# RWKV-7 steps: py in turn with pu, and a brought into the scores' bank by products

## The chip, the cores and the metric

The kernel runs on one core of a Trainium2 chip. A core has five engines, each with its own queue of instructions: TensorE (PE in the profile; its weight loads are shown apart as PEld), VectorE (DVE), ScalarE (ACT), GpSimd (POOL) and SyncE (SP), which issues most transfers. The metric is the device time of one execution in microseconds. The kernel before has a median of 1361.54 us over three runs (1357.82 to 1363.87).

## The reference

A two-layer decoder trunk works on 512 tokens of width 1024 in float32: a recurrent block (RG-LRU), a gated conv-MLP, an RWKV-7 time-mixing block, a second gated conv-MLP, and a final norm. The change lies in the RWKV-7 block, and there in the recurrence over tokens. For each of 16 heads with a 64x64 state S:

```python
    def step(S, inp):
        r_t, w_t, k_t, v_t, a_t, b_t = inp
        sa = jnp.einsum('bhij,bhj->bhi', S, a_t)
        S = S * w_t[:, :, None, :] + sa[..., None] * b_t[:, :, None, :] + v_t[..., :, None] * k_t[..., None, :]
        y = jnp.einsum('bhij,bhj->bhi', S, r_t)
        return S, y
```

So each token's output y is the state after its own update, read out by r; the state decays by w, is fed with the outer product of v and k, and is corrected along b by what it gives for a.

## The kernel before

The program is one long list of instructions, in the order in which a scheduler has put them on each engine. Large projections run as three fp32r products of 512 columns each (lines 51 to 53). The recurrence is not run token by token. The 512 tokens are cut into 8 chunks of 64; inside a chunk everything becomes products of 64x64 blocks (`rwkv_chunks`).

The heads lie in two halves H (eight heads each), and each half in two groups g of four heads. `step(n, ...)` runs for n = 0 to 16. Step n does chunk n of group 0 and chunk n - 1 of group 1, counted through both halves (0 to 15, so that steps 0 and 16 have one group alone). The parity q of a chunk says which 64 partitions it uses; the two groups of a step have opposite parities, and so use opposite halves of the partitions. A loop over `heads` goes i (0, 1), h (0, 1), group.

What one step computes, with the names of tiles that the profile shows:

- `pe`: the product of `W` (the scores and a) with the state `sv`, which also holds v in its other half. ScalarE copies it to `e1` (line 1200).
- `py`, first part (line 1206): r times the state. It opens an accumulation that the end of the step closes. r comes from `rts`, a copy on the right partitions, or from `AR`.
- `prep_s(n + 1)`: the next step's scores, `s` (line 1150): for each head the 128x128 block of (b, k) against (a, r), 64 rows deep. VectorE multiplies them by `masks` into `W` (line 1157). One 64x64 block of each result is not wanted, since the inverse of the solve holds it already.
- `between` and `fill(0)`: one part of a finished tail, and background products of other work.
- `pu` (line 1216): the inverse `LT` times `e1`. ScalarE copies it to `u`, a part of the tile `tu` (line 1220).
- `prep_t(n + 1)`: transposes of b and k (`tr`, line 1164), copied to `tok` (also in `tu`); then ScalarE puts a into the unwanted block of `W` (line 1173, one copy for each group and h), r into `rts` (line 1175), and v into `tu`.
- `fill(1)`, then `pd`: the change of the state, from `tok` and `u` (line 1229). VectorE adds it to the state and multiplies by the decay (lines 1237 to 1240).
- `py`, second part (line 1243): `W` times `u` and v. ScalarE copies y to `ytok` (line 1247). Then `fill(2)`.

Every second step starts a tail for 128 finished tokens: a norm over each head on VectorE, ScalarE and GpSimd (lines 1257 to 1271), and then four transposes `pz` on TensorE ahead of the next step's `pe`. Background work comes from three lists (`fills` gives how much of each is put in at the three places): products of v's projection and of the gate, the solve of the second half of the heads, whose VectorE chain (lines 1038 and 1040) runs through the first four steps, and the first half of the output projection.

All small products are in float32, and each shows as two records in the profile. `tile_position` gives the row and the column of the 128x128 array where a product's weights lie. The scores lie at rows h * 64 and take all columns; `py` and `pu` take one 64x64 quarter each, and the two groups take opposite quarters; `pe` and `pd` take all rows and half of the columns. All PSUM tiles come from one rotation of 8 banks. The scheduler may move an instruction past others of its engine; `keep_in_program_order` forbids it for the instruction that it is given.

Of the kernel before, what the change touches and what calls it, by code (L numbers as in the profile page):

```python
# [15 lines left out]
P = 128  # L16
# [5 lines left out]
C = 64  # L22
# [19 lines left out]
class Kernel:  # L42
# [1039 lines left out]
    def rwkv_chunks(self, pool, mv, AR, BK, PC, selk, LTs, again):  # L1082
# [9 lines left out]
        nc, tc, I = self.nc, self.tc, self.I  # L1092
        V = self.x.rearrange("p k t -> p (k t)").rearrange("p (c n) -> p c n", c=4)
        half = lambda i: slice(i * 64, i * 64 + 64)

        svs = [pool.tile([P, 4, 2, C], F32, name=f"sv{i}") for i in range(2)]
        rts = pool.tile([P, 4, C], F32, name="rts")
        e1 = pool.tile([P, 2, 2, C], F32, name="e1")
# [9 lines left out]
        for q in range(3):  # L1108
            for e in range(2):
                for z in range(2):  # L1110
                    m = masks[half(e), q, z, :]
                    nc.gpsimd.affine_select(m, m, [[1, C]], ALU.is_gt if z != q % 2 else ALU.is_ge, 0.0, base=0, channel_multiplier=-1)
        sets, ytok = {}, {}
# [28 lines left out]
        def prep_s(n):  # L1142
            gs = groups(n)
            W = sets[n][0]
            pss = [four(self.bank("s")) for _ in range(2)]
            for i in range(2):
                for g, bs, H, c, c2, q in gs:
                    ch = slice(q * P, (q + 1) * P)
                    for h in range(2):
                        nc.tensor.matmul(pss[h][:, 2 * g + i, :], BK[H][half(h), 2 * g + i, c2, ch], AR[H][half(h), 2 * g + i, c2, ch],  # L1150
                                         start=True, stop=True, tile_position=(h * 64, 0))

            q0, g0, k = gs[0][5], gs[0][0], len(gs)
            mask = masks[:, q0 : q0 + k].rearrange("p q z t -> p q (z t)").unsqueeze(2).to_broadcast([P, k, 2, P])
            two = lambda t: t[:, 2 * g0 : 2 * (g0 + k)].rearrange("p (g i) t -> p g i t", i=2)
            for h in range(2):
                nc.vector.tensor_tensor(two(W[:, h]), two(pss[h]), mask, ALU.mult)  # L1157
        def prep_t(n):
            gs = groups(n)
            W, tok, uv = sets[n]  # L1160
            pt = four(self.bank("tr"))
            for g, bs, H, c, c2, q in gs:
                for i in range(2 * g, 2 * g + 2):
                    nc.tensor.transpose(pt[:, i, :], BK[H][:, i, c2, q * P : (q + 1) * P], self.ident)
            bs = slice(gs[0][1].start, gs[-1][1].stop)
            nc.scalar.copy(tok[:, bs], pt[:, bs])
            for g, bs, H, c, c2, q in gs:
                bh = half(1 - q)
                for h in range(2):

                    part = lambda z: AR[H][half(h), bs, c2, q * P + z * C : q * P + (z + 1) * C]

                    tc.keep_in_program_order(nc.scalar.copy(W[bh, h, bs, bh], part(1 - q)))
                    if h == q:
                        nc.scalar.copy(rts[bh, bs], part(q))
                n0 = H * 512 + g * 256
                v = V[half(q), c2, n0 : n0 + 256].rearrange("p (i t) -> p i t", t=P)
                nc.scalar.copy(uv[half(q), bs], v)
                nc.vector.tensor_copy(svs[n % 2][half(q), bs].rearrange("p i h t -> p i (h t)"), v)
# [5 lines left out]
        def step(n, between):  # L1185
            gs = groups(n)
            W, tok, uv = sets.pop(n)
            sv = svs[n % 2]
            more = n < 2 * NC

            heads = [(i, h, G) for i in range(2) for h in range(2) for G in gs]
            by_head = lambda ps: ps[:, 0:256].rearrange("p (i h t) -> p i h t", h=2, t=C)
# [3 lines left out]
            for i, h, (g, bs, H, c, c2, q) in heads:  # L1196
                bh = half(1 - q)
# [1 line left out]
            of = slice(0, P) if len(gs) == 2 else half(1 - gs[0][5])  # L1199
            nc.scalar.copy(e1[of], pe[of])  # L1200

            py = by_head(self.bank("py"))
            for i, h, (g, bs, H, c, c2, q) in heads:
                kh, bh, b = half(q), half(1 - q), 2 * g + i
                r = rts[bh, b] if h == q else AR[H][bh, b, c2, q * P + q * C : q * P + q * C + C]
                nc.tensor.matmul(py[kh, i, h], r, sv[bh, b, h], start=i + h == 0, stop=False,  # L1206
                                 tile_position=(64 - q * 64, q * 64))
            if more:
                prep_begin(n + 1)
                prep_s(n + 1)  # L1210
            between()
            fill(0)
            pu = by_head(self.bank("pu"))
            for i, h, (g, bs, H, c, c2, q) in heads:
                bh = half(1 - q)
                nc.tensor.matmul(pu[bh, i, h], LTs[H][bh, c2 * 8 + (2 * g + i) * 2 + h, :], e1[bh, i, h], start=True, stop=True,
                                 tile_position=(64 - q * 64, 64 - q * 64))
            for g, bs, H, c, c2, q in gs:
                bh = half(1 - q)
                nc.scalar.copy(uv[bh, bs], flat(pu[bh]))  # L1220
            if more:
                prep_t(n + 1)
            fill(1)
            if any(c < NC - 1 for g, bs, H, c, c2, q in gs):
                pd = by_head(self.bank("pd"))
                for i, h, (g, bs, H, c, c2, q) in heads:
                    if c < NC - 1:
                        b = 2 * g + i
                        nc.tensor.matmul(pd[half(1 - q), i, h], tok[:, b, half(h)], uv[:, b, half(h)], start=True, stop=True, tile_position=(0, 64 - q * 64))
                for g, bs, H, c, c2, q in gs:  # L1230
                    if c == NC - 1:
                        continue
                    kh, bh = half(q), half(1 - q)
                    Sn = svs[1 - n % 2][kh, bs]
                    w = decay[:, H * 4 + 2 * g : H * 4 + 2 * g + 2, :, c : c + 1].to_broadcast([P, 2, 2, C])
# [5 lines left out]
            for i, h, (g, bs, H, c, c2, q) in heads:  # L1241
                kh, b = half(q), 2 * g + i
# [261 lines left out]
```

## Time and profile before

| | before |
|---|---|
| median of three runs | 1361.54 us |
| profiled execution, its own time | 1359.88 us |
| its span in the profile | 1357.9 us |
| granted TensorE clock, mean over the span | 0.989 |
| the 17 steps | about 744 to 914 us of the span |
| TensorE, VectorE, ScalarE busy over the span | 1324.4, 863.6, 632.6 us |
| copies of a into W (line 1173) | 64, median 297 ns |
| mask products into W (line 1157) | 34, median 680 ns |

The profile is one execution. The time outside its span is 2.0 us. A row of the timeline gives start, length, engine, line, operation and tiles (output <- inputs), with the number of instructions merged in it and, in brackets, the idle time before it and what ended it. The chain of waits is the work that ended last, followed back from the end: a shorter instruction shortens the program only if it, or what it releases, stands on that chain. A busy engine in a stretch is not for that reason the limit there.

### The profile page before, as it was taken

What the parts mean: (1) busy time and instruction counts of PE and PEld (TensorE: products, weight loads), DVE (VectorE), ACT (ScalarE), POOL (GpSimd) and SP (SyncE); (2) the same over time, 40 slices, a digit from 0 to 9 for tenths busy, and PEclk for the clock granted to TensorE, in tenths of its full rate; (3) what the DMA queues carried; (4) which work ended last, traced back from release to release, by engine and by line L of the source; (5) the groups of instructions that cost most, each with busy time, mean ns of one, the idle gap of its engine ahead of it and who ended that gap; (6) DMA issues with size and microseconds to landing.
All of it is one profiled execution on the core that took longest, in us unless ns stands there. A gap on an engine that the chain in (4) does not pass through costs nothing.

```text
span 1357.9 us, 19301 instructions
## 1 busy us (share of the span) xinstructions
PE 1324.4 (98%) x7827; PEld 1068.8 (79%) x7827; DVE 863.6 (64%) x1332; ACT 632.6 (47%) x1032; POOL 68.8 (5%) x113
## 2 busy tenths in 40 slices
PE   8999999999999999999999988898999999999998
PEld 7877888888888888866679776676888888888886
DVE  5988756555354755597897975776646464365623
ACT  6797534333233523378636578653634242244311
POOL 4000000000000000020011011110000000000000
PEclk8999999999999999999999989998999999999999
DMA  5423333232333434222121111212333222334311
GB/s 182 119 62 93 109 94 109 79 104 67 106 94 94 143 93 125 63 72 79 62 86 49 58 33 64 56 60 65 109 93 94 77 93 78 109 94 126 122 63 62
DMA packets 72120, 120.20 MB, mean 89 GB/s; under 512 B 9498, under 2 KB 21476, under 8 KB 71904
## 3 DMA queue, kind: packets, MB, share of 16 engines
q1 hardware_dynamic: 70672, 117.20, 27.9%
q8 instruction: 61, 1.00, 0.3%
q10 hardware_dynamic: 576, 1.05, 0.2%
q0 software_dynamic: 784, 0.74, 0.2%
q14 instruction: 27, 0.22, 0.1%
HBM read 114.44 MB, written 4.52 MB: 88 GB/s over the span
## 4 chain that ended last, share of the span: by engine, by line
PE 89%; DVE 6%; ACT 2%; issue 1%; DMA 1%; POOL 1%; SPq 0%; POOLq 0%; ACTq 0%; DVEq 0%
PE acc L51 22%; PE acc L53 22%; PE acc L52 22%; PE acc L616 3%; PE acc L615 3%; PE acc L617 3%; PE acc L986 1%; PE s L1150 1%; PE pe L1198 1%; PE acc L987 1%; PE py L1206 1%; PE acc L988 1%; DVE W L1157 1%; PE ssq L915 1%; DMA xin<-in_x_dram 1%
## 5 line engine op out<-in xcount | busy, mean ns | idle before, releaser
L51 PE MATMUL acc<-xs,wh 128*128 128x512 f32 x896 | 352.1, 393 | 0.0
L53 PE MATMUL acc<-xs,wl 128*128 128x512 f32 x896 | 349.0, 390 | 0.7 <-DVE wl L91 0.7
L52 PE MATMUL acc<-xs,wh 128*128 128x512 f32 x896 | 349.5, 390 | 0.0
L91 DVE TENSOR_TENSOR wl<-raw,wh 128x1024 fp32r<-128x1024 f32 (+1 forms) x201 | 242.6, 1215 | 164.6 <-PE acc L52 90.1
L90 ACT CAST wh<-raw 128x1024 fp32r<-128x1024 f32 (+1 forms) x201 | 208.1, 1045 | 258.6 <-DVE wl L91 167.6
L53 PEld LDWEIGHTS acc<-xs,wl 128*128 128x128 f32 x896 | 168.5, 188 | 36.5 <-DVE wl L91 1.2
L51 PEld LDWEIGHTS acc<-xs,wh 128*128 128x128 f32 x896 | 168.8, 188 | 35.0 <-ACT wh L90 0.2
L52 PEld LDWEIGHTS acc<-xs,wh 128*128 128x128 f32 x896 | 168.7, 188 | 34.7 <-DVE wl L91 0.2
L576 DVE SCALAR_TENSOR_TENSOR cv<-gpad,pv,cv 128x512 f32<-128x512 f32 x96 | 71.8, 748 | 22.6 <-ACT cv L574 21.5
L90 ACT CAST hid<-un 128x512 fp32r<-128x512 f32 x48 | 29.8, 620 | 109.2 <-DVE un L583 109.1
L616 PE MATMUL acc<-wh,hid 128*128 128x512 f32 (+1 forms) x200 | 76.8, 384 | 0.0
L615 PE MATMUL acc<-wh,hid 128*128 128x512 f32 (+1 forms) x200 | 76.5, 382 | 0.0
L617 PE MATMUL acc<-wl,hid 128*128 128x512 f32 (+1 forms) x200 | 75.9, 380 | 0.0
L52 PE MATMUL acc<-hid,wh 128*128 128x512 f32 x192 | 75.7, 394 | 0.0
L53 PE MATMUL acc<-hid,wl 128*128 128x512 f32 x192 | 75.6, 394 | 0.0
L51 PE MATMUL acc<-hid,wh 128*128 128x512 f32 x192 | 75.5, 393 | 0.0
L582 DVE TENSOR_TENSOR un<-acc,rb 128x512 f32<-128x512 f32 x48 | 33.0, 688 | 43.5 <-PE acc L53 43.5
L91 DVE TENSOR_TENSOR hid<-un,hid 128x512 fp32r<-128x512 f32 x48 | 33.1, 690 | 32.0 <-ACT hid L90 32.0
L574 ACT ACTIVATE cv<-gpad,pv 128x512 f32<-128x512 f32 x48 | 39.2, 817 | 20.1 <-DVE gpad L571 19.9
L578 ACT ACTIVATE ge<-cv 128x512 f32<-128x512 f32 x48 | 30.1, 627 | 35.9 <-DVE cv L576 35.9
L620 DVE TENSOR_TENSOR xtok<-xtok,acc 128x512 f32<-128x512 f32 (+1 forms) x25 | 16.6, 665 | 45.6 <-PE acc L617 45.6
L615 PEld LDWEIGHTS acc<-wh,hid 128*128 128x128 f32 x200 | 37.5, 188 | 8.0
(424 smaller groups left out, 2207.6 us busy)
## 6 DMA issues: line engine op xcount, KB each, us to landing
raw<-in_ffn_w_up_dram SPq DMA_DIRECT2D x96, 512.0 KB, 3.9
raw<-in_ffn_w_down_dram SPq DMA_DIRECT2D x48, 512.0 KB, 3.8
raw<-in_rwkv_w_rkv_dram SPq DMA_DIRECT2D x24, 512.0 KB, 3.8
raw<-in_lru_w_in_dram SPq DMA_DIRECT2D x16, 512.0 KB, 3.9
raw<-in_lru_w_out_dram SPq DMA_DIRECT2D x8, 512.0 KB, 3.7
raw<-in_rwkv_w_out_dram SPq DMA_DIRECT2D x8, 512.0 KB, 3.5
xd<-x SPq DMA_DIRECT2D x8, 256.0 KB, 2.0
AR<-xd SPq DMA_DIRECT2D x1, 2048.0 KB, 8.8
```

The source lines that it names most:

```text
L51: nc.tensor.matmul(ps, wh, xh, start=start, stop=False)
L52: nc.tensor.matmul(ps, wh, xl, start=False, stop=False)
L53: nc.tensor.matmul(ps, wl, xh, start=False, stop=stop)
L90: (self.nc.vector.tensor_copy if dve else self.nc.scalar.copy)(hi, src)
L91: self.nc.vector.tensor_tensor(lo, src, hi.bitcast(F32), ALU.subtract)
L574: nc.scalar.activation(cv, gp[:, 0:T], AF.Identity, bias=self.vec(f"ffn_conv_b{l}", fb), scale=cw(0))
L576: nc.vector.scalar_tensor_tensor(cv, gp[:, j : j + T], cw(j), cv, ALU.mult, ALU.add)
L578: nc.scalar.activation(ges[o], cv, AF.Gelu_apprx_tanh)
L582: nc.vector.tensor_tensor(un, ps, rbs[0], ALU.mult)
L615: nc.tensor.matmul(ps, hh[:, s], wh[:, k, m], start=kk == 0, stop=False)
L616: nc.tensor.matmul(ps, hl[:, s], wh[:, k, m], start=False, stop=False)
L617: nc.tensor.matmul(ps, hh[:, s], wl[:, k, m], start=False, stop=kk == 7)
```

## The change

It has four parts.

1. The scores are cut in three products for each head, each on one 64x64 quarter of the array. Part 0 (128 columns) makes the half of the rows that is wanted in full. Part 1 (64 columns) makes the one wanted block of the other half. Part 2 (64 columns) multiplies a by the identity, and so writes a itself into the block that was not wanted before. The loop goes round the quarters: for each i and part, over both groups and h.
2. The three mask regions that now lie over a stay at one, so that the mask product carries a into `W`. The 64 copies of a on ScalarE go. One copy of r for each group stays.
3. The first part of `py` no longer follows `pe`. Its products stand in turn with those of `pu`, and are kept in program order.
4. `py` takes its bank after `pu`, behind `fill(0)`.

```diff
@@ masks
             for e in range(2):
                 for z in range(2):
+                    if e == z == 1 - q % 2:
+                        continue
@@ prep_s
             for i in range(2):
-                for g, bs, H, c, c2, q in gs:
-                    ch = slice(q * P, (q + 1) * P)
-                    for h in range(2):
-                        nc.tensor.matmul(pss[h][:, 2 * g + i, :], BK[H][half(h), 2 * g + i, c2, ch], AR[H][half(h), 2 * g + i, c2, ch],
-                                         start=True, stop=True, tile_position=(h * 64, 0))
+                for part in range(3):
+                    for g, bs, H, c, c2, q in gs:
+                        for h in range(2):
+                            b, z = 2 * g + i, 1 - q if part else q
+                            row = slice(q * P + z * C, q * P + z * C + C)
+                            col = (slice(0, P), half(q), half(1 - q))[part]
+                            w = self.ident[half(h), half(h)] if part == 2 else BK[H][half(h), b, c2, row]
+                            nc.tensor.matmul(pss[h][half(z), b, col], w, AR[H][half(h), b, c2, q * P + col.start : q * P + col.stop],
+                                             start=True, stop=True, tile_position=(h * 64, z * 64))
@@ prep_t
-                for h in range(2):
-
-                    part = lambda z: AR[H][half(h), bs, c2, q * P + z * C : q * P + (z + 1) * C]
-
-                    tc.keep_in_program_order(nc.scalar.copy(W[bh, h, bs, bh], part(1 - q)))
-                    if h == q:
-                        nc.scalar.copy(rts[bh, bs], part(q))
+                nc.scalar.copy(rts[bh, bs], AR[H][half(q), bs, c2, q * P + q * C : q * P + (q + 1) * C])
@@ step
-            py = by_head(self.bank("py"))
-            for i, h, (g, bs, H, c, c2, q) in heads:
-                kh, bh, b = half(q), half(1 - q), 2 * g + i
-                r = rts[bh, b] if h == q else AR[H][bh, b, c2, q * P + q * C : q * P + q * C + C]
-                nc.tensor.matmul(py[kh, i, h], r, sv[bh, b, h], start=i + h == 0, stop=False,
-                                 tile_position=(64 - q * 64, q * 64))
             if more:
                 prep_begin(n + 1)
                 prep_s(n + 1)
             between()
             fill(0)
-            pu = by_head(self.bank("pu"))
+            pu, py = by_head(self.bank("pu")), by_head(self.bank("py"))
             for i, h, (g, bs, H, c, c2, q) in heads:
-                bh = half(1 - q)
-                nc.tensor.matmul(pu[bh, i, h], LTs[H][bh, c2 * 8 + (2 * g + i) * 2 + h, :], e1[bh, i, h], start=True, stop=True,
+                kh, bh, b = half(q), half(1 - q), 2 * g + i
+                nc.tensor.matmul(pu[bh, i, h], LTs[H][bh, c2 * 8 + b * 2 + h, :], e1[bh, i, h], start=True, stop=True,
                                  tile_position=(64 - q * 64, 64 - q * 64))
+                r = rts[bh, b] if h == q else AR[H][bh, b, c2, q * P + q * C : q * P + q * C + C]
+                tc.keep_in_program_order(nc.tensor.matmul(py[kh, i, h], r, sv[bh, b, h], start=i + h == 0, stop=False,
+                                                          tile_position=(64 - q * 64, q * 64)))
```

The scheduler moves instructions too. On TensorE in step 14, where no background product stands between the scores and `pu`, the rows from `pe` on are before:

```order
L1198 MATMUL pe<-sv_5482,W 64x64 x8
L1206 MATMUL py<-sv_5482,rts 64x64
L1206 MATMUL py<-sv_5482,AR_4343 64x64 x2
L1206 MATMUL py<-sv_5482,rts 64x64 x2
L1206 MATMUL py<-sv_5482,AR_4343 64x64 x2
L1206 MATMUL py<-sv_5482,rts 64x64
L1150 MATMUL s<-AR_4343,BK_4345 128x128 x8
L1216 MATMUL pu<-e_5485,LT_6776 64x64 x8
```

and with the change, to the first products of `pu`:

```order
L1200 MATMUL pe<-sv_5482,W 64x64 x8
L1157 MATMUL s<-AR_4343,BK_4345 64x128 x4
L1157 MATMUL s<-AR_4343,BK_4345 64x64 x4
L1157 MATMUL s<-AR_4343,ident 64x64 x4
L1157 MATMUL s<-AR_4343,BK_4345 64x128 x4
L1157 MATMUL s<-AR_4343,BK_4345 64x64 x4
L1157 MATMUL s<-AR_4343,ident 64x64 x4
L1213 MATMUL pu<-e_5485,LT_6851 64x64
L1216 MATMUL py<-sv_5482,rts 64x64
L1213 MATMUL pu<-e_5485,LT_6851 64x64
L1216 MATMUL py<-sv_5482,AR_4343 64x64
L1213 MATMUL pu<-e_5485,LT_6851 64x64
```

The eight products of `py` (16 records) have gone from behind `pe` to between those of `pu`, and the eight score products have become 24.

On ScalarE in step 10, from the copy of `e1` to the copy of y, before:

```order
L1200 COPY e_5485<-pe 128x256
L1175 COPY rts<-AR_4343 64x128 x2
L1178 COPY tu<-x 64x256 x2
L1173 COPY W<-AR_4343 64x2x64
L1220 COPY tu<-pu 64x256 x2
L1166 COPY tu<-tr 128x512
L1173 COPY W<-AR_4343 64x2x64 x3
L1247 COPY ytok<-py 64x256 x2
```

and with the change (some line numbers have moved by two to seven):

```order
L1202 COPY e_5485<-pe 128x256
L1180 COPY tu<-x 64x256 x2
L1177 COPY rts<-AR_4343 64x128
L1220 COPY tu<-pu 64x256 x2
L1173 COPY tu<-tr 128x512
L1177 COPY rts<-AR_4343 64x128
L1247 COPY ytok<-py 64x256 x2
```

The copies into `W` are gone, and one copy of r now stands ahead of the copy of u (`tu<-pu`), the other behind that of `tok` (`tu<-tr`). In step 6 the order on TensorE is another one: there all of `pu` comes first, then six products of the solve (`m1p`), and then all of `py`.

## The prediction

> **What bounds the kernel now.** I read the page first, then the steps' stretches, then the chain of waits, and last single steps. The page has shares over the whole program:
>
> ```profile
> span 1357.9 us, 19301 instructions
> PE 1324.4 (98%) x7827; PEld 1068.8 (79%) x7827; DVE 863.6 (64%) x1332; ACT 632.6 (47%) x1032; POOL 68.8 (5%) x113
> ```
>
> TensorE is nearly always busy, but the diff touches only the 17 steps, which run from about 744 to 914 us. The view by stretches (PE, PEld, DVE, ACT, POOL busy; granted clock; DMA) shows several limits there:
>
> ```profile
> 740.00:753.00 13.00, 13.00 (x228) 10.69 (x226) 12.14 (x31) 9.62 (x22) 0.00 (x0) 1.00 0.04 9
> 787.00:796.50 9.50, 9.50 (x130) 8.52 (x129) 4.27 (x9) 5.12 (x16) 0.00 (x0) 0.88 0.01 2
> 796.50:812.40 15.90, 13.38 (x180) 11.81 (x179) 13.76 (x22) 11.61 (x26) 1.64 (x1) 0.92 0.12 35
> 841.00:851.70 10.70, 6.06 (x96) 4.78 (x95) 7.16 (x14) 5.96 (x17) 1.63 (x1) 0.95 0.32 99
> 860.10:872.40 12.30, 10.04 (x123) 7.63 (x122) 10.85 (x19) 8.37 (x19) 3.60 (x3) 1.00 0.11 35
> ```
>
> Step 0 has VectorE busy 12.1 of 13.0 us; step 4 (third row) is all TensorE at a granted clock of 0.88; steps 5, 9 and 11 (the last three) leave TensorE idle, because the next step's transposes wait for the tail of a finished token pair:
>
> ```profile
> PE pz L1275 <- DVE ytok L1271: 10.8, 4, 3.8
> ```
>
> So a gain in TensorE's order counts only where the chain runs through it. The chain between 740 and 926 us, by line, and its pieces through step 8 (start, length, what):
>
> ```profile
> by line: PE pe L1198 6.1%; PE s L1150 6.1%; PE py L1206 5.5%; DVE W L1157 4.6%; issue 3.7%; PE acc L51 3.6%; POOL mu L1266 3.5%; PE pd L1229 3.4%; DVE DA L1038 3.4%; DVE sv L1238 3.3%; DVE X L1040 3.1%; PE acc L52 3.1%; PE acc L53 3.0%; PE
> ```
>
> ```profile
> 835.20 0.61 PE pe L1198 x16
> 835.82 0.61 PE py L1206 x16
> 836.43 1.14 PE s L1150 x16
> 837.57 0.68 DVE W L1157
> ...
> 838.27 0.30 ACT W L1173
> ...
> 838.60 0.38 ACT tu L1220
> ...
> 839.01 0.50 PE pd L1229 x5
> ```
>
> 5.5% of 186 us is 10.2 us of py on the chain, and 6.1% is 11.3 us of scores. In step 8 the chain leaves TensorE after the scores: the mask product, then a copy of a into W (L1173), which stands in ScalarE's queue ahead of the copy of u, which the state products (pd) need.
>
> **The change part by part.** *Speed of small products.* How long the new products take hangs on how many of the four 64x64 quarters of the array run at once. The timeline has all three cases (a product in fp32 is two records, so x16 is eight products):
>
> ```profile
> 747.44 0.67 PE L1216 MATMUL pu<-e,LT 64*64 64x64 f32 x8
> 837.45 0.68 PE L1216 MATMUL pu<-e,LT 64*64 64x64 f32 x16
> 724.10 0.46 PE L1017 MATMUL aab<-AR,BK 64*64 64x64 f32 x16
> L1017 PE MATMUL aab<-AR,BK x16: 218/218/267, 724.1 to 724.3; 64*64 64x64 f32 x16
> ```
>
> Without the last record's 0.22 us, step 0's pu on one quarter takes (0.67 - 0.22)/7 = 64 ns a record, step 8's on two quarters (0.68 - 0.22)/15 = 31 ns, and aab of the solve, which goes round all four, (0.46 - 0.22)/15 = 16 ns.
>
> *TensorE's order.* Today py, the scores and pu follow each other:
>
> ```profile
> 835.75 0.27 PE L1206 MATMUL py<-sv,rts 64*64 64x64 f32 x1
> 836.36 1.16 PE L1150 MATMUL s<-AR,BK 64*128 64x128 f32 x16
> ```
>
> From py's first record (835.75) to pu's last start (837.45 + 0.68 - 0.22 = 837.91) is 2.16 us, with a pause at each change of tile shape. Afterwards there are 48 records of scores and 32 of pu and py in turn, all 64x64 on four quarters. 16 of the 48 stream 128 columns; no row has these on quarters. Their bounds are 16 ns (weights decide) and 33 ns (columns decide: half of the 66 ns a record that the scores take now, (1.16 - 0.27)/15 = 59, rounded up with the pause). I take 32, twice the 64-column row, since all groups quoted scale with their columns. Sum: 16 x 32 + 32 x 16 + 32 x 16 = 1536 ns against 2160: **0.62 us a step**, as if py's slot vanished. The identity products, a third of the scores' records, cost 0.26 us of that.
>
> Which steps have it on the chain? The chain's pieces of py in steps 0, 1, 4, 5, 6, 10, 13 and 16 (start and length); steps 7, 12, 14 and 15 have step 8's 0.60 to 0.61, and steps 2, 3, 9 and 11 none worth showing:
>
> ```profile
> 744.91 0.60 PE py L1206 x8
> 753.70 0.52 PE py L1206 x12
> 788.05 1.05 PE py L1206 x16
> 798.21 0.54 PE py L1206 x12
> 815.94 0.92 PE py L1206 x14
> 852.83 1.05 PE py L1206 x16
> 880.97 0.52 PE py L1206 x12
> 909.53 0.60 PE py L1206 x8
> ```
>
> Steps 4 and 10 (1.05 each, in stretches of lower clock) scale to 0.62 x 1.05/0.61 = 1.07 each: 2.1 us. Steps 7, 8, 12, 14 and 16 give 5 x 0.62 = 3.1. In step 15 the scores are for step 16, which has one group and so two quarters: 8 x 62 + 16 x 31 = 1.0 us against about 0.5 now, which eats all but 0.1. Together 5.3 us. In steps 0, 1, 5 and 13 the chain goes to VectorE or ScalarE right behind py; of their 0.60 + 0.52 + 0.54 + 0.52 = 2.2 us I take half, 1.1, bounds 0 and 2.2. Step 6 gives nothing: there the order shows pu, then products of the solve, then py, no longer in turn.
>
> *ScalarE.* 64 copies (two for each of 32 group steps) of 0.30 us leave, 19 us of an engine that is not the bound; what counts is who stood behind them:
>
> ```profile
> 795.96 0.86 DVE L1238 TENSOR_TENSOR sv<-sv,decay 64x256 f32<-64x256 f32 x2
> 796.52 0.32 PE L1198 MATMUL pe<-sv,W 128*64 128x64 f32 x2
> 796.98 0.62 ACT L1173 COPY W<-AR 64x128 f32<-64x128 f32 x2
> 797.44 0.78 PE L1198 MATMUL pe<-sv,W 128*64 128x64 f32 x14
> 838.27 0.30 ACT L1173 COPY W<-AR 64x128 f32<-64x128 f32 x1 [0.50 <-DVE W L1157]
> 838.60 0.76 ACT L1220 COPY tu<-pu 64x256 f32<-64x256 f32 x2
> 840.27 0.23 PEld L1198 LDWEIGHTS pe<-sv,W 128*64 128x64 f32 x4 [0.25 <-ACT W L1173]
> L1198 PE MATMUL pe<-sv,W x16: 222/222/270, 840.3 to 841.7; 128*64 128x64 f32 x16
> 855.16 0.68 DVE W L1157
> 893.72 0.68 DVE W L1157
> ```
>
> In step 5 most of pe starts at 797.44 though the state's last multiplication ended at 795.96 + 0.86 = 796.82: 0.6 us. In step 9 pe waits for a copy at 840.27, and its 16 records then spread from 840.3 to 841.7, 1.4 us to the last start where step 8 took 0.5: 0.9 us. In steps 8, 10 and 14 (the two mask products on the chain, and step 8's) the copy of u starts 0.47 us after pu's end (837.45 + 0.68 = 838.13); without the copy about 0.05, so 3 x 0.42 = 1.3 us. Against this, the order puts one copy of r (rts, 0.30 us) ahead of u in steps 4, 7, 8, 10 and 12, and it waits for py, now as late as pu; it can begin some three pairs (0.2 us) before pu's end, so 0.15 us lost each, -0.75 (bounds 0 and -1.5). Sum: +2.05 us.
>
> *Nothing else.* VectorE has the same mask products, now over values that include a; ScalarE's copy of e1 keeps its cover: pu waits for it, and the scores' 1.0 us still run meanwhile, where a copy of this size takes 0.38 (u's piece above) and some 0.1 on either side. If ScalarE were late there by two such copies (0.76), each such step would lose about 0.3. The three mask regions left at one cost nothing in the steps.
>
> Total: 5.3 + 1.1 + 2.05 = **8.5 us**. The profiled execution took 1359.88 us, 1.7 under the median of 1361.54; it would take 1351.4, and the median **1353 us**, 0.62% less. Bounds of this case: with the 128-column records at 16 ns (0.26 us in eight steps, 2.1), all of the half-counted steps (1.1) and no loss to rts (0.75) the gain is 12.4; with none of the half-counted steps, rts at its worst, and VectorE's masks taking the copies' place for the 2.0, it is 4.6. Its own range is 1349 to 1357.
>
> The Trainium skill has two rules against this. "TensorE: Matmul & The Clock Gate" (section "Wait — 56ns, not 53.3ns?") has matmul starts never closer than about 25 ns: by it a step takes 16 x 33 + 64 x 25 = 2.13 us and TensorE's term is nothing. The trace disagrees, with 16 ns in aab. "TensorEngine Tiling (Array Packing)" (section "Gotcha 1: PSUM Pressure") says that different row tiles cannot access one PSUM bank at the same time; pu's bank, and now py's, is written by both row halves. The trace disagrees here too: with both halves pu takes 0.68 us for 16 records, with one half 0.67 for 8.
>
> **The rivals.** *Absorbed by VectorE and the tail.* Where the tail ends the step, TensorE's gain becomes a longer wait before pz. For it: the last three stretches above, and 10.8 us of such waits. Against it: the tail starts from the copy of y, which also comes earlier. If the gains in steps 4, 5, 8, 9 and 10 and the half-counted ones are lost, 5.3 - 2.1 - 0.62 + 0.42 for step 14 - 0.3 for rts = 2.7 us are left: **1359**. Longer waits may also lower the granted clock in further stretches: the 1.05 against 0.61 shows 0.4 us for each group of products.
>
> *Slower: only two quarters at a time.* If the new mixture (128 and 64 columns, three sources of weights) runs in pairs as pu and py do now, a step takes 16 x 62 + 64 x 31 = 2.98 us, 0.82 more than now. Over five full-clock steps, two at 1.7 times, step 15 and half of four this is 0.82 x 11.4 = 9.4 us, less the 2.05 of ScalarE: **1369**. It decides from a mean of 2160/96 = 22.5 ns a 64-column record on; aab's 16 speaks against it.
>
> *A floor, or one bank.* A floor under the distance of starts that takes all of TensorE's term leaves ScalarE's 2.05 us: 1359.5. If both row halves cannot write one bank together, pu and py take 32 x 31 = 0.99 instead of 0.51 us; 0.48 over the same steps without step 15 (10.4) is 5.0 lost: 1358. The rows of aab and pu contradict both. These are the two rules named above.
>
> *More.* VectorE's order starts earlier in every round, and the waits before pz shrink too: 13 us, 1348.
>
> **How the numbers follow.** Forecast 0.58, absorbed 0.27, pairs 0.06, floor or bank 0.04, more 0.05. A measurement tells about 0.5% (6.8 us) from no change; the three runs shown span 1357.82 to 1363.87. Of the forecast's 0.58, 0.49 lies beyond 6.8 us, with "more" 0.54 faster; the rest with absorbed and floor is 0.40 same; pairs 0.06 slower. The range 1346 to 1361 leaves out pairs, a tenth of absorbed and the tip of "more".
>
> **What would show it.** Right: in the steps after 787 us, py and pu as 32 records within about 0.75 us, the scores' 48 within 1.3; no ScalarE copy into W; u's copy within 0.2 us of pu's end in steps 8, 10, 14; py gone from the chain as a piece of its own. Wrong: 31 ns a record there; the same distance from step to step with longer waits of pz for L1271; lower clock in stretches that have 1.00 now; e1 late, with pu waiting for ScalarE.

## The result, and the profile after

The changed kernel takes **1352.58 us** (median of five runs, 1349.69 to 1354.45) against 1363.87 (five runs, 1357.82 to 1366.32): a ratio of **0.9917, 95% interval 0.9899 to 0.9935**. The forecast was 1353.0. Its profiled execution took 1353.01 us. The page of it, answering the first lines shown of before:

```profile
span 1351.3 us, 20246 instructions
PE 1315.4 (97%) x8339; PEld 1062.6 (79%) x8339; DVE 865.4 (64%) x1332; ACT 613.8 (45%) x968; POOL 67.8 (5%) x110
```

TensorE has 512 more records and 9 us less to do, ScalarE 64 copies and 19 us less. The timeline of step 8 (start, length, engine, line, operation, tiles, number):

```profile
833.62 0.69 PE L1200 MATMUL pe<-sv,W 128*64 128x64 f32 x16
834.23 0.56 PE L1157 MATMUL s<-AR,BK 64*64 64x128 f32 x16
834.61 0.30 PE L1157 MATMUL s<-AR,ident 64*64 64x64 f32 x8
834.73 0.51 PE L1157 MATMUL s<-AR,BK 64*64 64x128 f32 x16
835.07 0.30 PE L1157 MATMUL s<-AR,ident 64*64 64x64 f32 x8
835.18 0.22 PE L1216 MATMUL py<-sv,AR 64*64 64x64 f32 x1
835.19 0.23 PE L1213 MATMUL pu<-e,LT 64*64 64x64 f32 x2
...
835.61 0.22 PE L1216 MATMUL py<-sv,AR 64*64 64x64 f32 x1
```

The scores' 48 records start from 834.23 to 835.14, and pu and py's 32 records from 835.18 to 835.61, 0.43 us or 14 ns each. From the first to the last start the slot is 1.38 us, where it was 2.16; 1.54 was forecast. In the chain of waits of this step py no longer stands as a piece of its own (start, length, what):

```profile
834.30 1.06 PE s L1157 x48
835.36 0.04 PE py L1216
835.40 0.01 PE pu L1213 x2
...
835.75 0.30 ACT rts L1177
...
836.08 0.38 ACT tu L1220
```

After the products the chain still goes to ScalarE, now to the copy of r. The waits before pz, in the same view as before, and another row of that view:

```profile
PE pz L1275 <- DVE ytok L1271: 7.6, 5, 3.4
PE acc L986 <- ACT wh L90: 3.0, 1, 3.0
```

The fall from 10.8 to 7.6 us is no gain. In step 3 of the kernel before, 3.2 us of waiting stand before pz. In the changed kernel a product of a projection (acc) comes ahead of that pz, and waits 3.0 us for ScalarE. The other waits before pz make 7.6 us in both. One stretch got worse. The view by stretches around step 2 (PE, PEld, DVE, ACT, POOL busy; granted clock; DMA), first of the kernel before, then of the changed one, and last the timeline's row of pe of step 2 in each:

```profile
763.90:772.50 8.60, 8.54 (x129) 7.56 (x129) 8.04 (x21) 5.69 (x16) 1.28 (x1) 1.00 0.23 69
```

```profile
764.57:775.00 10.43, 10.43 (x160) 9.46 (x160) 9.26 (x23) 4.59 (x12) 1.18 (x1) 0.67 0.15 52
...
766.10:772.90 6.80, 6.80 (x88) 6.09 (x82) 5.99 (x14) 2.56 (x8) 1.18 (x1) 0.50 0.02 5
```

```profile
763.90 0.69 PE L1198 MATMUL pe<-sv,W 128*64 128x64 f32 x16 [0.63 <-DVE sv L1238]
764.57 0.69 PE L1200 MATMUL pe<-sv,W 128*64 128x64 f32 x16 [2.33 <-DVE sv L1238]
```

TensorE now stands idle for 2.33 us before pe of step 2, waiting for VectorE, where it had stood 0.63 us; then the clock falls to a half for 6.8 us.

### The profile page after: what moved, and what is told of

Read it like the earlier page. It is cut to its first block, busy times and chain, and to the rows that moved or that the text cites. A ratio compares the mean times of both kernels' runs of the same rounds, so it can differ in the third digit from the quotient of the medians.

```text
span 1351.3 us, 20246 instructions
## 1 busy us (share of the span) xinstructions
PE 1315.4 (97%) x8339; PEld 1062.6 (79%) x8339; DVE 865.4 (64%) x1332; ACT 613.8 (45%) x968; POOL 67.8 (5%) x110
## 3 DMA queue, kind: packets, MB, share of 16 engines
q10 hardware_dynamic: 576, 1.05, 0.2%
## 4 chain that ended last, share of the span: by engine, by line
PE 89%; DVE 5%; ACT 3%; issue 1%; POOL 1%; DMA 1%; SPq 0%; POOLq 0%; ACTq 0%; DVEq 0%
PE acc L51 22%; PE acc L52 22%; PE acc L53 22%; PE acc L616 3%; PE acc L615 3%; PE acc L617 3%; PE acc L986 1%; PE s L1157 1%; PE acc L987 1%; PE acc L988 1%; PE pe L1200 1%; PE ssq L915 1%; PE pd L1229 1%; POOL mu L1266 1%; DMA xin<-in_x_dram 1%
```

## The experiments

The runs were made in three groups, each with its own runs of the kernel before: medians 1364.18 (13 runs), 1361.01 (23) and 1361.84 us (11). Ratios are to these; kernels of one group are compared by their medians. The expectations give 3.7 us as the length of the stretches at half clock. That was misread: the rows show 3.4, 6.8 and 10.2 us.

**The two kernels once more.** The changed kernel ran again in the first and in the third group, the kernel before with a profile in the third.

> The changed kernel once more, as the measure for the others of this group. By the comparison of the two traces: steps 4 to 16 are shorter by about 8.7 us together, and steps 1 to 3 longer by 2.5 us, since TensorE stood idle for 2.3 us before pe of step 2 and then ran 3.7 us at half clock. If that loss belongs to the changed kernel, the trace shows it again and the time stays 9 to 11 us under the kernel before; if it was an accident of one execution, step 2 (pe to the next pe) takes 8.6 us as before instead of 10.4 and the profiled time is about 2 us lower.

> The changed kernel on the chip of this group, as the measure for the two that follow: 9 to 12 us under the kernel before, u's copy 0.25 us behind pu's end in steps 8 and 10.

> The kernel before, once more with a profile: the runs of it spread from 1355 to 1366 us, while those of the changed kernel lie within 1350 to 1354, and the profile that the prediction worked from took 1359.9. Theory (the spread comes from where the granted clock falls to a half, which differs between executions): the same order and the same waits, the stretches at half clock at other places or of other lengths, their sum (21 us between 740 and 930 us before) explaining the difference in time at about half a microsecond for each. Rival (another cause): the same half-clock stretches, the difference in another place.

Measured: 1350.93 us (four runs; 0.9909, 0.9896 to 0.9921) and 1352.52 (0.9926, 0.9906 to 0.9946); the kernel before took 1359.14 in its profiled execution. The length of a step, from the first start of pe to the next (and from pe of step 16 to the end), in two traces of before and three of after:

| step | before | after |
|---|---|---|
| 0 | 8.79, 8.79 | 8.16, 8.16, 8.16 |
| 1 | 10.88, 10.87 | 11.95, 11.95, 11.95 |
| 2 | 8.60, 9.48 | 10.43, 10.45, 9.03 |
| 3 | 14.43, 14.00 | 14.05, 13.33, 14.18 |
| 4 | 9.59, 8.61 | 9.72, 8.07, 9.99 |
| 5, 6 | 27.79, 27.81 | 25.58, 28.36, 25.59 |
| 7 | 10.83, 10.83 | 9.27, 9.28, 9.28 |
| 8 | 5.17, 5.17 | 4.08, 4.07, 4.07 |
| 9, 10 | 19.79, 19.79 | 18.32, 17.96, 18.49 |
| 11 | 12.26, 12.26 | 12.36, 12.36, 14.09 |
| 12 | 7.93, 7.93 | 7.41, 7.41, 7.42 |
| 13 | 10.65, 10.64 | 10.65, 10.65, 10.65 |
| 14 | 8.65, 8.64 | 7.50, 7.48, 7.49 |
| 15 | 9.27, 9.27 | 8.73, 8.73, 8.72 |
| 16 and the rest | 449.05, 449.02 | 448.63, 448.42, 448.12 |
| sum | 613.7, 613.1 | 606.8, 606.7, 607.2 |

The gain from the first step to the end is 6.5 us in the traces, and the loss in steps 1 to 3 recurs in all three. Where one kernel's steps differ between executions, the clock does. The stretch from 740 to 930 us in the two traces of before (one fence) and in the three of after (the next):

```profile
740.00:930.00 190.00, 168.53 (x2324) 134.09 (x2323) 141.39 (x273) 121.34 (x306) 25.06 (x20) 0.95 0.17 52
740.00:930.00 190.00, 167.70 (x2326) 133.39 (x2325) 142.82 (x274) 121.17 (x306) 24.82 (x20) 0.96 0.16 52
```

```profile
740.00:930.00 190.00, 166.19 (x2849) 132.89 (x2844) 144.87 (x277) 104.34 (x246) 25.04 (x20) 0.92 0.17 52
740.00:930.00 190.00, 166.08 (x2844) 132.41 (x2841) 144.34 (x278) 104.47 (x246) 25.13 (x20) 0.92 0.17 52
740.00:930.00 190.00, 166.92 (x2836) 133.54 (x2830) 143.80 (x277) 103.91 (x246) 24.93 (x20) 0.91 0.16 52
```

Clocks of 0.95 and 0.96 are 19 and 15 us at half clock (190 x 0.05 x 2), 0.92 and 0.91 are 30 and 34: the traces of after carry some 15 us more of it than those of before. About 2 of these the window makes, since the last stretch of before runs on past 930 us (in the first trace to 932.6). The runs without a trace show what that is worth. In the first group eight of the 13 runs of before have a mean granted clock of 0.983 or 0.984 and take 1362.28 to 1364.92 us, and one at 0.994 takes 1356.27, some 8 us for 0.011. That is about 30 us of half clock (1360 x 0.011 x 2), so 0.27 us for each and not the half that was expected. Time and clock thus go together, as the theory has it; where the clock falls in the longer runs of before is not known, since both its profiles (0.989 and 0.992) are of shorter ones. Set on one clock, the 6.5 us of the traces (after at 0.986, 0.988 and 0.985, a mean 0.0042 lower) become about 6.5 + 0.0042 x 8/0.011 = 9.6, an estimate. Runs at 0.988 and 0.989 in the first and third group say the same: six of before lie at 1359.68 to 1361.94, six of the changed kernel at 1349.79 to 1352.36, about 10 us apart. The 11.3 us between the first medians would then be these 10 and a little of the clock; of those five runs of before, the clock of only one is known.

**The parts apart.** First py in turn with pu alone, on the kernel before (the loop of py behind pe goes):

```diff
-            py = by_head(self.bank("py"))
...
+            pu, py = by_head(self.bank("pu")), by_head(self.bank("py"))
             for i, h, (g, bs, H, c, c2, q) in heads:
                 nc.tensor.matmul(pu[bh, i, h], ...)
+                tc.keep_in_program_order(nc.tensor.matmul(py[kh, i, h], r, sv[bh, b, h], ...))
```

> Only the second half of the change: the kernel before, with the products of py in turn with those of pu; scores on 128 columns and copies of a into W as before. Theory (TensorE's slots count): py's slot of 0.6 us vanishes in the steps that had it on the chain, the scores stay at 1.14 us: 10.4 weighted steps x 0.55 = 5.7 us faster than the kernel before, or a little less, because the copies of a still stand ahead of u's copy on ScalarE. Rival (the copies are what mattered): within 2 us of the kernel before. Rival (only the whole chain counts, since ScalarE's copies take over where py leaves): about 3 us faster.

Then the products of a alone: the changed kernel with the loop of py moved back behind pe.

```diff
+            py = by_head(self.bank("py"))
...
                 nc.tensor.matmul(pu[bh, i, h], ...)
-                tc.keep_in_program_order(nc.tensor.matmul(py[kh, i, h], r, sv[bh, b, h], ...))
```

> Only the first half of the change: scores in quarters, a by identity products, no copies of a into W; py at its old place behind pe and pu alone. Theory: the scores' 48 records take 0.91 to 1.02 us against 1.14, 0.12 to 0.25 us x 10 weighted steps = 1.2 to 2.6, and ScalarE's copies 2 us: 3.2 to 4.6 us faster than the kernel before; with the run of py in turn alone the two parts add up to the whole, 9 to 11 us. Rival (the copies are what mattered): nearly all of the gain, 8 us or more. Rival (only py's slot counts): within 1 us of the kernel before.

And the changed kernel with py and pu at the same place, but as two loops:

```diff
             for i, h, (g, bs, H, c, c2, q) in heads:
-                nc.tensor.matmul(pu[bh, i, h], ...)
                 tc.keep_in_program_order(nc.tensor.matmul(py[kh, i, h], ...))
+            for i, h, (g, bs, H, c, c2, q) in heads:
+                tc.keep_in_program_order(nc.tensor.matmul(pu[bh, i, h], ...))
```

> The changed kernel, but py and pu at the same place as two loops, first all of py, then all of pu, so that only two quarters of the array work at a time. Theory (quarters at once set the time): 32 records at 31 ns = 0.99 us instead of 0.65 with the last record, about 0.4 us in each of some 10.4 weighted steps: 4 to 5 us slower than the changed kernel. Rival (it is the place of py, beside pu and without a change of tile shape between, and not the turn): within 1 us of the changed kernel, and 32 records in about 0.7 us.

| | median us | ratio to before (95%) | slot of step 8, us | u's copy behind pu's end in step 8 |
|---|---|---|---|---|
| before | 1364.18 | | 2.17 | 0.46 |
| py in turn alone | 1358.70 | 0.9967 (0.9955 to 0.9979) | 1.57 | 0.66 |
| products of a alone | 1353.65 | 0.9930 (0.9917 to 0.9943) | 1.78 | 0.05 |
| two loops | 1354.12 | 0.9929 (0.9917 to 0.9941) | 1.68 | 0.26 |
| changed | 1350.93 | 0.9909 (0.9896 to 0.9921) | 1.38 | 0.25 |

Each part alone is worth a good deal, 5.5 and 10.5 us, and together they are worth 13.3, not 16. Part of that is the clock. The products of a ran at 0.988 and 0.989, and lie some 8 us under the three runs of before at 0.988 (1361.70 to 1361.94). Py in turn has the mean clock of before, 0.986, and a mean of 1358.99 us against 1362.64, so 4 us. At one clock the parts are thus about 8 and 4 us, and the whole about 10, by estimate. On TensorE they overlap by a pause: with the scores in 64x64 quarters no change of tile shape is left between py, scores and pu. Step 8 with the products of a alone:

```profile
829.98 0.27 PE L1208 MATMUL py<-sv,rts 64*64 64x64 f32 x1
...
830.39 0.33 PE L1157 MATMUL s<-AR,BK 64*64 64x128 f32 x2
...
831.35 0.63 PE L1218 MATMUL pu<-e,LT 64*64 64x64 f32 x15
```

py takes 0.41 us up to the scores, where it took 0.61 (835.75 to 836.36), though it still runs on two quarters; the 0.2 us were the pause, and so py in turn has only the rest to win. Two loops cost 3.2 us against the changed kernel, 0.30 us in step 8; some 0.7 of the 3.2 may be the clock (0.987 against 0.988 on the mean). The expectation was 4 to 5, from 0.4 a step. The first products of pu start at 835.62, before py's last at 835.78, so the loops overlap:

```profile
835.35 0.22 PE L1214 MATMUL py<-sv,AR 64*64 64x64 f32 x1
...
835.62 0.27 PE L1218 MATMUL pu<-e,LT 64*64 64x64 f32 x2
```

With only the place kept, the slot of step 8 is 1.68 us against 1.38: the turn counts too. With py in turn alone, ScalarE takes part of the gain back. Its step 8:

```profile
837.60 0.30 ACT L1173 COPY W<-AR 64x128 f32<-64x128 f32 x1 [0.56 <-DVE W L1157]
837.80 0.29 ACT L1175 COPY rts<-AR 64x128 f32<-64x128 f32 x1
838.12 0.76 ACT L1218 COPY tu<-pu 64x256 f32<-64x256 f32 x2
```

pu ends 0.6 us earlier than it would have, and u's copy waits longer: the copy of a ahead of it has to wait for VectorE's mask product.

**The copies kept.** The changed kernel with the copies of a back on ScalarE:

```diff
-                nc.scalar.copy(rts[bh, bs], AR[H][half(q), bs, c2, q * P + q * C : q * P + (q + 1) * C])
+                for h in range(2):
+                    part = lambda z: AR[H][half(h), bs, c2, q * P + z * C : q * P + (z + 1) * C]
+                    tc.keep_in_program_order(nc.scalar.copy(W[bh, h, bs, bh], part(1 - q)))
+                    if h == q:
+                        nc.scalar.copy(rts[bh, bs], part(q))
```

> The changed kernel, but with the 64 copies of a into W kept on ScalarE (they write once more what the mask product already put there). TensorE's work is that of the changed kernel, ScalarE's that of the kernel before. Theory of the prediction (the copies are worth 2.05 us, with 0.75 of it lost to the copies of r): 2 to 3 us slower than the changed kernel. Rival, after the run of py in turn alone, which gained only about half as much as the run of the products of a alone: without the copies gone, the copy of u falls behind by 0.4 to 0.8 us in steps 8, 10 and 14 and by more in others, and most of the slot's gain is lost: 5 to 7 us slower, u's copy 0.6 us or more behind pu's end in steps 8 and 14.

Measured: 1356.69 us (12 runs, 0.9970, 0.9951 to 0.9989), 4.1 above the 1352.57 of the next kernel, which does what the changed kernel does. That lies between the two theories, at twice the 2.05 of the prediction. By the spread of the 12 and the six runs it is uncertain by some 2 us either way. Against the kernel before, the 0.9970 is no more of a gain than the 0.9967 of py in turn alone, in another group: while the copies stay, the shorter scores win nothing that can be told from zero. The products of a pay by what they take out of ScalarE's queue. u's copy is 0.65 us behind pu's end in step 8, 1.00 in step 14, and in step 7 the trace shows what holds it:

```profile
827.65 0.30 ACT L1181 COPY W<-AR 64x128 f32<-64x128 f32 x1 [1.44 <-DVE W L1164]
827.86 1.16 ACT L1079 COPY LT<-ltp 32x512 f32<-32x512 f32 x2
829.03 0.29 ACT L1181 COPY W<-AR 64x128 f32<-64x128 f32 x1
829.33 0.74 ACT L1226 COPY tu<-pu 64x256 f32<-64x256 f32 x2
```

The copy of a waits 1.44 us for the mask product, and behind it stand copies of the solve and u: 2.48 us after pu's end at 826.86. The kernel before has the same queue in step 7:

```profile
829.09 0.30 ACT L1173 COPY W<-AR 64x128 f32<-64x128 f32 x1 [0.69 <-DVE W L1157]
829.69 0.29 ACT L1173 COPY W<-AR 64x128 f32<-64x128 f32 x1 [0.30 <-DVE W L1157]
830.00 1.16 ACT L1079 COPY LT<-ltp 32x512 f32<-32x512 f32 x2
831.17 0.74 ACT L1220 COPY tu<-pu 64x256 f32<-64x256 f32 x2
```

**The copy of r.** Two buffers first, then kept in program order:

```diff
-        rts = pool.tile([P, 4, C], F32, name="rts")
+        rtss = [pool.tile([P, 4, C], F32, name=f"rts{i}") for i in range(2)]
```

```diff
-                nc.scalar.copy(rts[bh, bs], ...)
+                tc.keep_in_program_order(nc.scalar.copy(rts[bh, bs], ...))
```

> The changed kernel with the copy of r in two buffers, in turn from step to step, so that it no longer waits for py. The order of the engines is the same. Theory (the copy of r, which now waits for py, holds u's copy up): u's copy starts 0.05 us behind pu's end in steps 1, 3, 4, 8, 10 and 13, where it now starts 0.25 to 0.28 behind it, 0.2 x 6 = 1.2 us faster than the changed kernel, of which the steps that VectorE or the tail bounds keep up to half. Rival (no effect on the chain): within 0.5 us, with u's copy early all the same.

> The changed kernel with the copy of r kept in program order on ScalarE. With two buffers nothing had changed, since the order moved the copy a step ahead and it waited for the same py; kept in order, the copy has no wait for TensorE left. Theory (the copy of r holds u's copy up where it waits for py): u's copy 0.05 us behind pu's end in steps 1, 3, 10 and 13 instead of 0.25 to 0.28, 0.2 us each, at most 1 us faster than the changed kernel. Rival (it costs nothing, since VectorE or the tail sets those steps): within 0.5 us.

Two buffers gave 1352.57 us (0.9927, 0.9900 to 0.9955) and the same delays of u to 0.01 us: with a buffer free, the scheduler moved the copy one step ahead, and it waits for the same py. The experiment did not take the wait away. Kept in order, the copy has no wait on TensorE. Step 3 of the changed kernel, and of this one:

```profile
778.23 0.30 ACT L1177 COPY rts<-AR 64x128 f32<-64x128 f32 x1 [1.16 <-PE py L1216]
778.55 0.76 ACT L1220 COPY tu<-pu 64x256 f32<-64x256 f32 x2
```

```profile
777.51 0.76 ACT L1220 COPY tu<-pu 64x256 f32<-64x256 f32 x2 [1.27 <-PE pu L1213]
```

u's copy now starts 0.06 us behind pu's end in steps 1, 3 and 13 and 0.07 in step 10 (0.25 to 0.28 before). The time is 1351.63 us against 1352.52 of the changed kernel in the same group (ratios 0.9923 and 0.9926, with intervals that overlap): up to 0.9 us, not told from nothing. In step 8 the delay only falls to 0.20. There ScalarE is at work without a break from e1 on, with copies of v (0.82 us) and of r (0.30) ahead of u.

**The square on VectorE.** In steps 9 and 11 of the changed kernel u's copy is 2.1 and 2.3 us late, behind the tail's square, which waits for VectorE:

```profile
840.30 0.63 ACT L1260 ACTIVATE ysq<-ytok 128x512 f32<-128x512 f32 x1 [1.42 <-DVE ytok L1258]
...
841.66 0.30 ACT L1177 COPY rts<-AR 64x128 f32<-64x128 f32 x1
841.98 0.76 ACT L1220 COPY tu<-pu 64x256 f32<-64x256 f32 x2
```

```diff
-            nc.scalar.activation(sq, y, AF.Square)
+            nc.vector.tensor_tensor(sq, y, y, ALU.mult)
```

> The changed kernel with the tail's square on VectorE instead of ScalarE. In the changed kernel the copy of u starts 2.1 to 2.3 us behind pu's end in steps 9 and 11, since the square stands ahead of it and waits for VectorE. Theory (these steps end with the tail, so u's delay costs nothing): u's copy starts within 0.1 us in steps 9 and 11, and the time stays within 1 us, minus 0.2 us a tail for the two handovers saved, plus 0.67 us a tail of VectorE's time where VectorE is the limit. Rival (u's delay counts): about 2 us gained in each of the two steps, 3 to 4 us faster than the changed kernel.

Neither held: 1360.17 us (12 runs; 0.9988, 0.9971 to 1.0004), 7.6 slower than the kernel with two buffers of r in its group. u's copy does come 0.27 us behind pu's end in steps 9 and 11, and yet these steps take 11.19 and 13.16 us against 10.58 and 12.36: u's delay had cost little or nothing there, because VectorE's tail ends the step. Step 7 grows from 9.28 to 13.20: a product of the bonus, which stands in TensorE's queue ahead of the state's products, now waits 2.0 us for VectorE, and half clock follows:

```profile
PE bon L1294 <- DVE pr L1292: 2.0, 1, 2.0
```

**The clock.** Idle products where TensorE waits, which write into a bank that the next products overwrite (behind the last pz, into a bank of their own). First at three places, ahead of pe of step 2 and of pz of the fourth and of the last tail; then, with the copy of r kept in order, ahead of pz of the fourth and of the last tail, of pd of steps 9 and 11, and behind the last pz. The lines of the tails, the same in both:

```diff
...
             pz = self.bank("pz")
+            for i in range({(0, 3): 24, (1, 3): 20}.get((H, c2), 0)):
+                tc.keep_in_program_order(nc.tensor.transpose(pz[:, i % 4 * P : (i % 4 + 1) * P], self.ident, self.ident))
             for i in range(4):
...
```

> The changed kernel with idle products (transposes of the identity into the bank that the next products overwrite) at three places where TensorE waits: 14 ahead of pe of step 2, 24 ahead of pz of the fourth tail, 20 ahead of pz of the last. Theory (the half clock follows TensorE's idle time): the granted clock stays at 1.00 behind these three places, step 2 takes 8.6 us as before the change instead of 10.4, and the program is 3 to 5 us faster than the changed kernel (half of three stretches of 3.7 us, less what other engines bound). Rival (the lower clock is not due to idle time, or those stretches wait for VectorE anyway): stretches at half clock at the same places, or gone without gain, within 1 us.

> The changed kernel with the copy of r kept in program order, and with idle products (transposes of the identity) ahead of pz of the fourth and the last tail (24 and 20), of pd of steps 9 and 11 (12 each) and behind the last pz (12); none in step 2, where VectorE is the limit. Theory (the clock falls after TensorE's idle time, and the final projections lose about half of each stretch): full clock from 843 to 870 us and from 918 us on, 2.5 to 4 us faster than the changed kernel. Rival (the clock falls elsewhere instead, as it did behind the idle time of step 3 when step 2 was filled): half-clock stretches of the same sum at other places, within 1 us.

The first gave 1349.04 us (0.9905, 0.9876 to 0.9933; 1352.57 for the kernel with two buffers of r in its group), but step 2 won nothing: full clock there, and VectorE kept pe of step 3 to 775.81 us, with TensorE idle for 3.79 us ahead of it and half clock after. This trace is of the slowest of its six runs (1353.24 us at 0.988; the others take 1347.93 to 1349.36 at 0.991 to 0.993), so that what the others gained is not seen in it. The second took **1348.52 us** (six runs, 1345.76 to 1350.99; ratio 0.9899, 0.9878 to 0.9920), 4.0 less than the changed kernel in its group (1352.52). The idle products alone are worth 3.1, against the kernel that only keeps the copy of r in order (1351.63). It is the lowest median of all, though not told from the first (0.9905). Three of its runs lie at 1345.76 to 1346.88 with clocks of 0.992 to 0.994, three at 1350.17 to 1350.99 with 0.989; the trace is one of the fast three. Step 10 and the stretch around the last pz in that changed kernel, then in this one:

```profile
846.61:854.52 7.91, 7.82 (x141) 6.45 (x140) 3.81 (x9) 4.80 (x14) 0.00 (x0) 0.78 0.29 87
912.00:926.00 14.00, 9.19 (x33) 6.88 (x32) 8.10 (x13) 3.56 (x8) 0.30 (x1) 0.76 0.13 39
```

```profile
843.95:850.18 6.23, 6.23 (x140) 4.95 (x140) 3.80 (x9) 4.38 (x13) 0.00 (x0) 1.00 0.41 120
909.00:923.00 14.00, 12.77 (x73) 10.39 (x72) 8.46 (x14) 4.12 (x9) 0.00 (x0) 1.00 0.06 22
```

Step 10 takes 6.23 instead of 7.91 us, and step 16 with the rest 446.42 instead of 448.12. But step 12 takes 9.71 instead of 7.42, with 3.4 us at half clock in it. Both theories had something: in these traces the half clock is gone where the idle time is filled, and the gain stays if TensorE is the limit behind it; where VectorE is the limit, the idle time and the half clock turn up a step later, and one stretch turns up elsewhere. Where the clock falls in the three longer runs is not known.

## Why the prediction was right, and where it was not

**The forecast** of 8.5 us (1353 for the median) met 1352.58, but not term by term, and the closeness is in part luck: with two more runs the median of before moved from 1361.54 to 1363.87, so that 11.3 us were measured between the medians, not 8.5. TensorE's and ScalarE's terms were both too small, steps 1 to 3 lost where nothing or a gain was forecast, and the errors nearly cancel: 6.5 us in the traces as they stand, about 10 at one clock.

**Speed on four quarters: right.** 0.62 us a step was forecast, 0.78 measured in step 8. The 64-column records take 14 ns, not 16. The scores take 0.95 us up to the first py where 1.02 was forecast, so (0.95 - 32 x 0.014)/16 = 31 ns is left for a 128-column record (32 taken). The rival of two quarters at a time (22.5 ns and more) falls, and so do those of a floor and of one bank. The Trainium skill, "TensorE: Matmul & The Clock Gate" (section "Wait — 56ns, not 53.3ns?"), has starts never closer than about 25 ns; the trace disagrees, with 14. By the Trainium skill, "TensorEngine Tiling (Array Packing)" (section "Gotcha 1: PSUM Pressure"), different row tiles cannot access one PSUM bank at the same time; here products from both row halves write pu's and py's banks in turn without loss, each half on its own 64 partitions.

**Step 15: mis-sized.** The scores for the lone group of step 16 were put at 1.0 us, for two quarters. Their 24 records start within 0.48 us, and the step gained 0.54 where 0.1 was forecast:

```profile
894.55 0.44 PE L1157 MATMUL s<-AR,BK 64*64 64x128 f32 x8
...
895.17 0.50 PE L51 MATMUL acc<-BK,wh 128*128 128x512 f32 x1
```

**ScalarE: mis-sized, by half.** 2.05 us were forecast, 4.1 measured. The step that failed counted u's delay in three steps (8, 10, 14) and pe's in two. The copies of a chain ScalarE's queue to VectorE's masks in more steps, step 7 among them (forecast 0.47, measured 1.55), and the earlier pu comes, the longer u waits for them. In the kernel before, these copies waited 9.9 us in all for the mask products; with the copies kept in the changed kernel it is 13.7. The two terms were thus not independent: with the copies kept, TensorE's new order is worth 4.3 us (1361.01 to 1356.69, both at a mean clock of 0.988), where 5.3 and 1.1 were booked for it. In steps 8 and 10 u's copy starts 0.25 us behind pu's end, not within 0.2, since the copy of r holds it up, at about the 0.15 forecast; in step 14 it is 0.06.

**VectorE's steps: wrong sign.** Half of py's pieces in steps 0, 1, 5 and 13 were put down as gain, 1.1 us, and nothing for 2 and 3. Step 0 gained 0.63, step 13 nothing, and steps 1 to 3 lost 0.8 to 2.5 us, 1.6 on the mean (before 33.9 and 34.4, after 36.4, 35.7 and 35.2). Steps 5 and 6 together took 2.2 us less in two traces and 0.6 more in the third, where 10.2 us of half clock fall in them, so that step 5's part stays open. Step 1 is VectorE's work from end to end in both traces. The view by stretches has step 1 before and after:

```profile
753.02:763.90 10.88, 10.25 (x126) 6.67 (x125) 10.29 (x24) 6.54 (x16) 0.00 (x0) 1.00 0.20 69
```

```profile
752.63:764.57 11.94, 9.62 (x157) 6.16 (x157) 11.24 (x27) 5.38 (x12) 0.00 (x0) 1.00 0.25 69
```

VectorE does 27 instructions (11.24 us) between two pe where it did 24 (10.29): the order puts more pieces of the solve's chain (lines 1038 and 1040, about 0.45 us each) ahead of the state's last product. Two of the three are pieces that step 0, ending earlier, had left, so its gain is given back: steps 0 and 1 together take 19.67 us before and 20.11 after, one piece more. The time that TensorE saved became the wait of 2.33 us, and the wait the half clock. This is the sentence of the rival "absorbed", that longer waits may lower the granted clock in further stretches, and the sign "lower clock in stretches that have 1.00 now"; it came true in steps 1 to 3 alone, and the rest of that rival did not: in steps 8, 9, 10 and 14 the gain stayed.

**Steps 4 and 10: mis-sized.** They were scaled by the lower clock of their stretches to 1.07 us of TensorE's gain each. (The row of step 4 in the prediction's view by stretches is the second, 787.00 to 796.50, not the third.) In step 4 the clock differs from one execution to the next: it takes 8.61 before and 8.07 after where both have full clock, 0.54 us, and 9.59 and 9.72 where both have not. There the scaling rested on an accident of one trace. In step 10 a part is at half clock in all five traces (mean clocks of 0.86 and 0.85 before, 0.80, 0.85 and 0.78 after): it takes 8.39 and 8.42 us before and 7.74, 7.37 and 7.91 after, 0.5 to 1.05 us gained where 1.34 were booked (1.07, and 0.42 - 0.15 of ScalarE).

## What to carry to other kernels

Products on 64x64 quarters should go round all four, with one tile shape from group to group: the turn and the missing pauses are both visible in a row of the timeline. Before a gain is booked on one engine, look at what stands ahead of the next instruction on the engine that takes over, and whom that waits for; a small copy that needs VectorE's result can hold a whole chain. A wait that TensorE gains in front of a step is paid for twice if the clock falls behind it, and idle products that fill it are worth a try where TensorE is the limit afterwards.

## What the runs showed of the hardware

The half clock comes in stretches of 3.4, 6.8 and 10.2 us, and in the traces above each beside a wait of TensorE. Two rows show one of 3.4 us (the changed kernel in the third group) and one of 10.2 us (in the first group); that of 6.8 us stands above:

```profile
764.80:768.20 3.40, 3.40 (x58) 3.17 (x50) 3.17 (x9) 1.24 (x4) 1.05 (x1) 0.50 0.13 49
```

```profile
809.50:819.70 10.20, 10.20 (x181) 8.24 (x181) 5.58 (x9) 4.92 (x12) 0.00 (x0) 0.50 0.02 4
```

The same wait of 2.3 us before step 2 was followed by 6.8 us in two traces and by 3.4 in the third. Not each wait is followed by any: the 3.2 us in step 3 of the kernel before were followed by 3.4 us at half clock in one trace and by full clock in the other. The Trainium skill, "TensorE: Matmul & The Clock Gate", section "What's actually happening", has a free-running activity window of about 3.4 us; the multiples agree with it, and a window that runs free would explain why executions of one kernel differ. The same page of the Trainium skill, section "HAM oscillation — how this bites in real kernels", warns of idle gaps above about 3.4 us; here 2.3 us were enough.

A product from the other row half, into the other 64 partitions of the same bank and in turn, costs nothing that shows: 32 records of pu and py start 14 ns apart.
